# RWKV time mixing on one core: larger packets for the cast loads, and one store a batch for batches 2 to 9

## The chip, the cores and the metric

The kernel runs on one core of a Trainium2 chip. The metric is the device time of one execution in microseconds; for the kernel before it is the median of three runs, 203.77 us (203.05 to 205.11). The profile is of one execution of 203.05 us. Its span, from the first to the last instruction, is 201.3 us. All places in time below are counted from the start of that span.

## The reference: what is computed

The input x has 16 batches of 2048 rows of 256 float32 values. Each row is mixed with the row before it by three vectors of weights, projected by 256 x 256 matrices, gated by a sigmoid and projected once more:

```python
x_prev[:, 1:, :] = x[:, :-1, :]          # zero for the first row of a batch
xv = x * time_mix_v + x_prev * (1 - time_mix_v)
xr = x * time_mix_r + x_prev * (1 - time_mix_r)
v = xv @ value_weight
r = xr @ receptance_weight
out = (1 / (1 + exp(-r)) * v) @ output_weight
```

The reference also computes a key projection that does not reach the output; the kernel leaves it out. x is 33.55 MB, and so is the output: 2 MB each way for a batch.

## The kernel before

A batch is four units of 512 rows, so there are 64 units. For each unit the kernel brings x into the layout with the features on partitions (xt), mixes it with its shifted copy (mix), and multiplies: receptance (psum_r), value (psum_v), then, one unit later, the output projection of the gated product (psum_o). Each of these is a few matmuls on TensorE. ScalarE takes the sigmoid, copies the transposed x out of PSUM (xt) and copies the finished output (o_sb). VectorE adds and multiplies, GpSimd scales. The last 18 units and two blocks of batch 11 get their xt from DMA transposes, not from TensorE.

The buffers that matter here:

```python
xpool = ctx.enter_context(tc.tile_pool(name="xpool", bufs=6))
...
opool = ctx.enter_context(tc.tile_pool(name="opool", bufs=3))
ps_t_pool = ctx.enter_context(tc.tile_pool(name="ps_t", bufs=2, space=bass.MemoryType.PSUM))
ps_v_pool = ctx.enter_context(tc.tile_pool(name="ps_v", bufs=1, space=bass.MemoryType.PSUM))
ps_r_pool = ctx.enter_context(tc.tile_pool(name="ps_r", bufs=1, space=bass.MemoryType.PSUM))
ps_o_pool = ctx.enter_context(tc.tile_pool(name="ps_o", bufs=1, space=bass.MemoryType.PSUM))
...
x_unit = opool.tile([P, 3, UJ, D], FP32, name="o_sb")   # the first user of an output buffer
```

So six batches of x (bf16) can be in the core at once, and three batches of output (float32). An output buffer is taken by x_unit first, and then by the batches in turn: batch 0 takes the second, batch 1 the third, batch 2 the one of x_unit, batch 3 that of batch 0, batch 4 that of batch 1.

The loads. They cast from float32 to bf16 on the way and are issued by GpSimd. In batches 2 to 15 a partition holds 16 neighbouring rows of x, which are 16 KB in a row in memory; `max_dma_last_dim=8192` cuts them into two packets. Batches 0 and 1 are laid out by units (4 KB in a row).

```python
def rows(b):
    return x[b].rearrange("(p j) d -> p j d", p=P)

def unit_rows(t, b, e, n=1):
    return t[b, e * TU : (e + n) * TU, :].rearrange("(e p j) d -> p e j d", p=P, j=UJ)

def load(b):
    if b not in x_bf:
        x_bf[b] = xpool.tile([P, J, D], BF16, name="x_bf")
    if b < BYUNIT:                     # BYUNIT = 2
        for e in range(UB):
            nc.gpsimd.dma_start(
                out=x_bf[b][:, e * UJ : (e + 1) * UJ, :], in_=unit_rows(x, b, e)[:, 0]
            )
        return
    return nc.gpsimd.dma_start(out=x_bf[b], in_=rows(b), max_dma_last_dim=8192)
```

When loads go out. The load of batch b + 5 is issued where batch b begins to be transposed:

```python
            if b == 1 and e > 0:
                load(b + e + 1)
            elif b > 1 and e == 0 and b + 5 < B:
                if b == 2:
                    load(6)
                last_load = load(b + 5)
```

The output of a unit, and its store on SyncE. In batches 0 and 1 two units go out in one DMA, in pieces of 4 KB; after that two units go out in pieces of 8 KB; the last eight units go out one by one or in parts:

```python
def store(queue, b, lo, hi):
    dst = out[b].rearrange("(p j) d -> p j d", p=P)
    queue.dma_start(out=dst[:, lo:hi, :], in_=o_sb[b][:, lo:hi, :])

def output(g, z):
    b, e = divmod(g, UB)               # UB = 4 units a batch
    if e == 0:
        o_sb[b] = opool.tile([P, J, D], FP32, name="o_sb")
    j0 = e * UJ
    if g >= NU - 4:
        ...                            # the last units, in parts
        return
    ps = ps_o_pool.tile([P, UJ, D], FP32, name="psum_o")
    for jj in range(UJ):
        out_matmuls(ps, z, jj, jj)
    nc.scalar.copy(out=o_sb[b][:, j0 : j0 + UJ, :], in_=ps)     # line 335
    if b < BYUNIT:
        if e % 2 == 1:
            nc.sync.dma_start(
                out=unit_rows(out, b, e - 1, 2),
                in_=o_sb[b][:, j0 - UJ : j0 + UJ, :].rearrange("p (e j) d -> p e j d", j=UJ),
            )
    elif g >= NU - 8:
        store(nc.sync, b, j0, j0 + UJ)
    elif e % 2 == 1:
        store(nc.sync, b, j0 - UJ, j0 + UJ)
```

The order in the loop over units, cut to what matters. CROSS is 40:

```python
for g in range(NU - 1):
    ...
    project(ps_r, g, 0)                # receptance
    nc.scalar.activation(out=s_sb, in_=ps_r, func=ACT.Sigmoid)
    if g == CROSS:
        for e in (1, 2):
            by_dma(B - 5, e * UJ, (e + 1) * UJ, last_load)      # DMA transposes, after the last load
    advance(...)                       # loads and transposes of later units
    ...
    project(ps_v, g, 1)                # value
    nc.vector.tensor_tensor(out=z_sb, in0=s_sb, in1=ps_v, op=ALU.mult)
    ...
    output(g - 1, z_prev)              # from g = 41 on: output(g - 2), ahead of the value part
```

Of the kernel before, what the change touches and what calls it, by code (L numbers as in the profile page):

```python
# [15 lines left out]
def kernel(  # L16
# [25 lines left out]
    nc = tc.nc  # L42
# [4 lines left out]
    J = S // P  # L47
    UJ = 4
    TU = UJ * P
    UB = J // UJ  # L50
# [5 lines left out]
    CROSS = NU - BYDMA - LOOK  # L56
# [23 lines left out]
    x_bf = {}  # L80
# [12 lines left out]
# [13 lines that stand above are left out]
                    out=x_bf[b][:, e * UJ : (e + 1) * UJ, :], in_=unit_rows(x, b, e)[:, 0]  # L106
                )
            return
        return nc.gpsimd.dma_start(out=x_bf[b], in_=rows(b), max_dma_last_dim=8192)  # L109

    x_unit = opool.tile([P, 3, UJ, D], FP32, name="o_sb")
    tm_rows = consts.tile([2 * KO, P], FP32)
# [1 line left out]
    for m, tm in enumerate([time_mix_r, time_mix_v]):  # L114
        nc.scalar.dma_start(
            out=tm_rows[m * KO : (m + 1) * KO, :], in_=tm.rearrange("(ko p) -> ko p", p=P)
        )
    for h in (1, 0):
        nc.sync.dma_start(
            out=x_unit[:, 0, h * H : (h + 1) * H], in_=unit_rows(x, 0, 0)[:, 0, h * H : (h + 1) * H, :]  # L120
        )
    nc.sync.dma_start(
        out=w_f32[:, 0], in_=receptance_weight.rearrange("(ko p) n -> p ko n", p=P)
# [12 lines left out]
    nc.gpsimd.dma_start(out=x_bf3, in_=unit_rows(x, 0, 3)[:, 0])  # L136
    nc.gpsimd.dma_start(out=wo_bf, in_=output_weight.rearrange("(ko p) n -> p ko n", p=P))
    load(1)
    load(2)

    def warm_up(n):
# [159 lines left out]
    def out_matmuls(ps, z, jj, slot):  # L301
        for ko in range(KO):
            nc.tensor.matmul(  # L303
                out=ps[:, slot, :],
                lhsT=z[:, ko, jj * P : (jj + 1) * P],
                rhs=wo_bf[:, ko, :],
                start=(ko == 0),
                stop=(ko == KO - 1),
# [6 lines that stand above are left out]
    def out_part(pool, name, z, b, e, jj, n, copy, queue):  # L315
        ps = pool.tile([P, n, D], FP32, name=name)
        for k in range(n):
            out_matmuls(ps, z, jj + k, k)
        lo = e * UJ + jj
        copy(out=o_sb[b][:, lo : lo + n, :], in_=ps)  # L320
        store(queue, b, lo, lo + n)

    def output(g, z):
        b, e = divmod(g, UB)
# [4 lines that stand above are left out]
            for h, (pool, name) in enumerate([(ps_t_pool, "ps_t"), (ps_o_pool, "psum_o")]):  # L329
                out_part(pool, name, z, b, e, h * H, H, nc.scalar.copy, nc.sync)  # L330
# [4 lines that stand above are left out]
        nc.scalar.copy(out=o_sb[b][:, j0 : j0 + UJ, :], in_=ps)  # L335
# [5 lines that stand above are left out]
                )  # L341
        elif g >= NU - 8:
            store(nc.sync, b, j0, j0 + UJ)
        elif e % 2 == 1:
            store(nc.sync, b, j0 - UJ, j0 + UJ)

# [68 lines left out]
    def advance(limit):  # L415
        nonlocal tnext, last_load
        while tnext <= min(limit, NU - 1):
            b, e = divmod(tnext, UB)
# [6 lines that stand above are left out]
            if tnext < NU - BYDMA:  # L425
                transposes(tnext)
            tnext += 1

    first_transposes()
    for ko in range(KO):  # L430
        nc.vector.tensor_scalar(
            out=w_prev[:, ko, :],
# [6 lines left out]
        out=w_bf[:, 0, 0, :], in0=w_f32[:, 0, 0, :], scalar1=tms[:, 0, 0:1], scalar2=None, op0=ALU.mult  # L439
    )  # L440
    nc.scalar.activation(
        out=w_bf[:, 0, 1, :], in_=w_f32[:, 0, 1, :], func=ACT.Copy, scale=tms[:, 0, 1:2]
# [3 lines left out]
    for ko in range(KO):  # L446
        nc.vector.tensor_scalar(
            out=w_bf[:, 1, ko, :],
# [50 lines left out]
    for g in range(NU - 1):  # L499
# [23 lines left out]
        if LATE_O < g < NU - 2:  # L523
            output(g - 2, z_prev2)
# [29 lines left out]
        if z_prev is not None and not LATE_O <= g < NU - 3:  # L554
            output(g - 1, z_prev)
# [34 lines left out]
```

## Time and profile before

| | us |
|---|---|
| time, median of three runs | 203.77 |
| span in the profile | 201.3 |
| TensorE matmuls busy | 195.9 (97%) |
| VectorE busy | 186.7 (93%) |
| ScalarE busy | 180.9 (90%) |
| GpSimd busy | 83.3 (41%) |
| 14 loads of a batch (1024 KB of bf16 each): issue to landing, median | 27.1 |
| 28 stores of 1024 KB: issue to landing, median | 9.5 |

The busy time of an engine is the time in which one of its instructions was under way; matmuls overlap, so a busy TensorE can still be short of its peak. The page's second part cuts the span into 40 slices of 5 us and gives each a digit in tenths. The waits list, per engine and line, what ended an engine's idle time, with the total, the number of times and the longest one. A store's or load's time to landing runs from its issue to the last of its bytes, so it holds the time in the queue as well. Sizes of loads are those written, in bf16; as many bytes again are read, since the source is float32.

### The profile page before, as it was taken

The page shows a single profiled execution, that of the slowest core. Times are in us where ns is not written, and L with a number is a line of the kernel's source. Part 1 is how long each engine was busy: PE and PEld are TensorE (multiplying, and loading weights), DVE is VectorE, ACT ScalarE, POOL GpSimd, SP SyncE. Part 2 cuts the span into 40 slices and gives each one's busy share as a digit, 9 for nine tenths or more (in the row PEclk, how much of TensorE's full clock was granted, in tenths as well). Part 3 has the DMA queues.
Part 4 walks back from the last instruction along what each step waited for, and adds up shares of the span by engine and source line. Part 5 has one row for each costly group of instructions (what it writes and reads, how often), then busy time and mean ns, then how long its engine had stood idle before and what let it go on. Part 6 is the DMA issues. An engine that isn't in the chain of part 4 may idle for free.

```text
span 201.3 us, 3922 instructions
## 1 busy us (share of the span) xinstructions
PE 195.9 (97%) x1436; PEld 127.1 (63%) x1436; DVE 186.7 (93%) x301; ACT 180.9 (90%) x202; POOL 83.3 (41%) x109
## 2 busy tenths in 40 slices
PE   7999999999999999999999999999999999999992
PEld 7766676666666666666666666665656565555671
DVE  2899999999999999999999999999999999999963
ACT  2699899999999999999999999989999999999982
POOL 1754543462542644434462543434344444444200
PEclk9999999999999999999999999999999999999999
DMA  5999999999999999999999999989999999997575
GB/s 187 282 177 217 237 281 274 276 283 273 298 313 309 315 311 304 291 316 298 289 295 291 300 313 295 300 310 181 297 170 405 241 349 254 280 417 314 212 311 210
DMA packets 31130, 56.74 MB, mean 282 GB/s; under 512 B 19716, under 2 KB 21000, under 8 KB 28040
## 3 DMA queue, kind: packets, MB, share of 16 engines
q1 hardware_dynamic: 26160, 40.24, 59.2%
q0 software_dynamic: 4800, 16.12, 40.5%
q8 instruction: 11, 0.18, 0.3%
q10 hardware_dynamic: 152, 0.13, 0.2%
q14 instruction: 7, 0.06, 0.1%
HBM read 34.34 MB, written 33.55 MB: 337 GB/s over the span
## 4 chain that ended last, share of the span: by engine, by line
PE 83%; ACT 5%; DMA 5%; issue 3%; DVE 2%; SPq 0%; POOL 0%; DVEq 0%; ACTq 0%
PE psum_o L303 25%; PE psum_v L279 24%; PE psum_r L279 24%; PE ps_t L200 8%; DMA x_bf<-in_x_dram 3%; DMA w_f<-n_receptance_weight_dram 2%; ACT s_sb L512 2%; ACT mix L491 1%; ACT o_sb L335 1%; ACT xt L216 1%; DVE mix L271 1%; DVE z_sb L549 1%; DVE mix L249 1%; PE ps_t L303 1%; PE ps_t L279 0%
## 5 line engine op out<-in xcount | busy, mean ns | idle before, releaser
L259 POOL TENSOR_SCALAR mix<-xt,c_sb 128x1024 bf16<-128x1024 bf16 (+1 forms) x55 | 61.0, 1109 | 91.8 <-DVE mix L271 80.9
L549 DVE TENSOR_TENSOR z_sb<-s_sb,psum_v 128x1024 bf16<-128x1024 bf16 x63 | 76.6, 1217 | 3.6 <-PE psum_v L279 1.5
L271 DVE TENSOR_TENSOR mix<-mix,xt 128x1024 bf16<-128x1024 bf16 x112 | 77.3, 698 | 1.7
L279 PEld LDWEIGHTS <-w_bf 128*128 128x128 bf16 x516 | 48.7, 98 | 37.9 <-issue 0.7
L512 ACT ACTIVATE s_sb<-psum_r 128x1024 bf16<-128x1024 f32 x63 | 65.0, 1032 | 3.4 <-PE psum_r L279 2.7
L335 ACT COPY o_sb<-psum_o 128x1024 f32<-128x1024 f32 x60 | 61.1, 1018 | 7.5 <-PE psum_o L303 7.5
L279 PE MATMUL psum_v<-mix,w_bf 128*128 128x512 bf16 (+1 forms) x256 | 65.3, 377 | 0.3 <-DVE z_sb L549 0.2
L303 PE MATMUL psum_o<-wo_bf,z_sb 128*128 128x256 bf16 x494 | 64.4, 272 | 0.1
L279 PE MATMUL psum_r<-mix,w_bf 128*128 128x512 bf16 (+1 forms) x252 | 64.3, 377 | 0.1
L303 PEld LDWEIGHTS <-z_sb 128*128 128x128 bf16 x512 | 49.9, 98 | 20.7 <-issue 1.5
L216 ACT COPY xt<-ps_t 128x1024 bf16<-128x1024 bf16 x38 | 38.7, 1029 | 0.0
L200 PEld LDWEIGHTS <-x_bf 128*128 128x128 bf16 x344 | 22.5, 98 | 9.7 <-POOL xt_first L407 0.7
L200 PE MATMUL ps_t<-ident,x_bf 128*128 128x128 bf16 x344 | 25.7, 219 | 0.2 <-DMA x_bf<-in_x_dram 0.2
L249 DVE TENSOR_SCALAR mix<-xt,c_sb 128x1024 bf16<-128x1024 bf16 (+1 forms) x50 | 22.5, 459 | 0.0
L491 ACT ACTIVATE mix<-xt,c_sb 128x1024 bf16<-128x1024 bf16 x11 | 12.7, 1158 | 0.0
L109 POOL DMA_DIRECT2D x_bf<-in_x_dram x14 | 10.5, 749 | 0.0
L271 DVE TENSOR_TENSOR mix<-mix,xt_first 128x1024 bf16<-128x1024 bf16 x15 | 10.2, 686 | 0.1
L259 POOL TENSOR_SCALAR mix<-xt_first,c_sb 128x512 bf16<-128x512 bf16 x6 | 4.1, 686 | 8.3 <-DVE xt_first L408 8.2
L249 DVE TENSOR_SCALAR mix<-xt_first,c_sb 128x512 bf16<-128x512 bf16 x22 | 6.7, 355 | 0.2
L216 ACT COPY xt_first<-ps_t 128x1024 bf16<-128x1024 bf16 x5 | 5.1, 1029 | 0.0
L144 PE MATMUL ps_t<-zeros 128*128 128x128 bf16 x31 | 3.7, 313 | 1.0 <-DVE zeros L87 1.0
L144 PEld LDWEIGHTS <-zeros 128*128 128x128 bf16 x31 | 3.3, 148 | 1.0 <-DVE zeros L87 1.0
(64 smaller groups left out, 48.4 us busy)
## 6 DMA issues: line engine op xcount, KB each, us to landing
out_dram<-o_sb SPq DMA_DIRECT2D x28, 1024.0 KB, 9.5
x_bf<-in_x_dram POOLq DMA_DIRECT2D x14, 1024.0 KB, 27.1
out_dram<-o_sb SPq DMA_DIRECT2D x4, 512.0 KB, 2.7
out_dram<-o_sb SPq DMA_DIRECT2D x6, 256.0 KB, 2.5
x_bf<-in_x_dram POOLq DMA_DIRECT2D x5, 256.0 KB, 6.9
o_sb<-in_x_dram SPq DMA_DIRECT2D x2, 512.0 KB, 4.8
o_sb<-in_x_dram SPq DMA_DIRECT2D x2, 256.0 KB, 2.9
out_dram<-o_sb SPq DMA_DIRECT2D x3, 128.0 KB, 2.0
```

Of the source, the lines that this page charges most:

```text
L109: return nc.gpsimd.dma_start(out=x_bf[b], in_=rows(b), max_dma_last_dim=8192)
L200: nc.tensor.transpose(out=ps[:, jj], in_=src[:, jj, ko * P : (ko + 1) * P], identity=idn)
L216: nc.scalar.copy(out=xt[b][:, j0 : j0 + UJ], in_=ps)
L249: nc.vector.tensor_scalar(out=mixed(piece)[:, :, ko], in0=xt[b][:, slots(piece), ko], scalar1=c_sb[:, m, ko : ko + 1], scalar2=None, op0=A ...
L259: op = nc.gpsimd.tensor_scalar(out=mixed(piece)[:, :, 1], in0=xt[b][:, slots(piece), 1], scalar1=c_sb[:, m, 1:2], scalar2=1.0, op0=ALU.mul ...
L271: return nc.vector.tensor_tensor(out=mixed(piece), in0=mixed(piece), in1=xt[b][:, slots(piece, 1)], op=ALU.add)
L279: nc.tensor.matmul(out=ps[:, mo, :], lhsT=w_bf[:, m, ko, mo * P : (mo + 1) * P], rhs=mixed((b, m, e * TU + lo, e * TU + hi))[:, :, ko], st ...
L303: nc.tensor.matmul(out=ps[:, slot, :], lhsT=z[:, ko, jj * P : (jj + 1) * P], rhs=wo_bf[:, ko, :], start=(ko == 0), stop=(ko == KO - 1),)
L335: nc.scalar.copy(out=o_sb[b][:, j0 : j0 + UJ, :], in_=ps)
L491: nc.scalar.activation(out=mixed(piece)[:, :, ko], in_=xt[b][:, slots(piece), ko], func=ACT.Copy, scale=c_sb[:, m, ko : ko + 1],)
L512: nc.scalar.activation(out=s_sb, in_=ps_r, func=ACT.Sigmoid)
L549: nc.vector.tensor_tensor(out=z_sb, in0=s_sb, in1=ps_v, op=ALU.mult)
```

## The change

The loads of batches 2 to 15 are no longer cut: a partition's 16 KB go in one packet (8 KB written). The outputs of batches 2 to 9 are stored once a batch, when the last of its four units has been copied, so that a partition's 16 KB go in one packet as well. The purpose is to have fewer and larger packets, each of which has a fixed part of its own. Batches 0 and 1 and batches 10 to 15 are stored as before.

```diff
-        return nc.gpsimd.dma_start(out=x_bf[b], in_=rows(b), max_dma_last_dim=8192)
+        return nc.gpsimd.dma_start(out=x_bf[b], in_=rows(b), max_dma_last_dim=16384)
...
         elif g >= NU - 8:
             store(nc.sync, b, j0, j0 + UJ)
+        elif g < CROSS:
+            if e == UB - 1:
+                store(nc.sync, b, 0, J)
         elif e % 2 == 1:
             store(nc.sync, b, j0 - UJ, j0 + UJ)
```

## The prediction

> **What bounds the kernel now.** I read the page's busy shares first, then the chain that ended last, the waits, the DMA queues by stretch, and last the timeline around one output copy. From the page:
>
> ```profile
> PE 195.9 (97%) x1436; PEld 127.1 (63%) x1436; DVE 186.7 (93%) x301; ACT 180.9 (90%) x202; POOL 83.3 (41%) x109
> ...
> PEclk9999999999999999999999999999999999999999
> DMA  5999999999999999999999999989999999997575
> ...
> PE 83%; ACT 5%; DMA 5%; issue 3%; DVE 2%; SPq 0%; POOL 0%; DVEq 0%; ACTq 0%
> ```
>
> TensorE is busy for 97% of the span at full clock and carries 83% of the chain, so nothing can be gained where it already runs without a gap. But the second row of digits says that the DMA engines are full too, from 5 to about 180 us. In the waits, TensorE lost almost nothing to them:
>
> ```profile
> PE ps_t L200 <- DMA x_bf<-in_x_dram: 0.2, 1, 0.2
> ```
>
> So there are two full resources side by side, and DMA is hidden only by buffers: six for loads, three for outputs. The question is what the change does to the order in which the DMA engines serve the two queues, and whether a buffer then comes free too late. Here are the queues in two stretches, 36 to 48 us and 60 to 72 us (queue, packets, MB, share of 16 engines; q0 carries the loads issued on GpSimd, q1 the stores issued on SyncE):
>
> ```profile
> DMA packets 868, 3.34 MB, mean 278 GB/s; under 512 B 56, under 2 KB 56, under 8 KB 867
> q0 software_dynamic: 432, 1.67, 68.6%
> q1 hardware_dynamic: 435, 1.65, 36.3%
> ...
> q0 software_dynamic: 337, 1.27, 52.4%
> q1 hardware_dynamic: 335, 2.48, 51.2%
> ```
>
> In the first stretch the load packets (8 KB read, 4 KB written as bf16) meet the 4 KB stores of batches 0 and 1; in the second they meet the 8 KB stores of later batches. In both, the packet **counts** are equal (432 to 435, 337 to 335), while the shares of time are 2:1 and then 1:1. The engines take one packet of each queue in turn, whatever its size. This is the fact on which my prediction rests.
>
> The third reading is how late outputs and loads land. The store of the second half of batch 1 goes out at 39.7 us, and the load of batch 10 at 54.4 us:
>
> ```profile
> L338 SPq DMA_DIRECT2D out_dram<-o_sb x1: 373/373/373, 39.7 to 39.7; - x1
> DMA to landing us min/median/max: 14.8/14.8/14.8
> ...
> L109 POOL DMA_DIRECT2D x_bf<-in_x_dram x1: 757/757/757, 54.4 to 54.4; - x1
> DMA to landing us min/median/max: 36.4/36.4/36.4
> ```
>
> The store lands at 54.5 us. Its buffer's next user is the first output copy of batch 4 (three output buffers in rotation, x_unit being the first user of one):
>
> ```profile
> L335 ACTq EVENT_SEMAPHORE  x1: 38/38/38, 64.2 to 64.2; - x1
> ...
> 65.91 1.01 ACT L335 COPY o_sb<-psum_o 128x1024 f32<-128x1024 f32 x1 [0.20 <-PE psum_o L303]
> ...
> 67.88 1.04 PE L303 MATMUL psum_o<-wo_bf,z_sb 128*128 128x256 bf16 x8
> ```
>
> The wait instruction stands once per batch ahead of its first copy, so I take it to cover all stores from the old buffer. The copy starts at 65.91 us, 11.4 us after the store landed: that is today's margin. The third line is TensorE's next use of the same PSUM buffer, at 67.88 us. The copy ends at 66.92, so TensorE gives it only 0.96 us of slack.
>
> **What the Trainium skill says.** "DMA: Bandwidth & Descriptors", section Queues, rings and completion order: each DMA engine goes round its queue rows packet by packet. The trace agrees, with the counts above. That page puts several descriptors into a typical packet; here the equal counts show that the turn passes after each 4 or 8 KB piece. Section Rules for kernel authors of that page wants at least 1 MiB a DMA for bandwidth; the loads and most stores have that already, so there is little left to gain from larger ones. Section Issuing engines are not separate DMA queues: the queues run on the same 16 engines. The shares above, 68.6 and 36.3% in one stretch, agree.
>
> **The change part by part.** First the price of a packet. In 36 to 48 us, q0 has 1.67 MB in 4 KB pieces, 408 packets, for 68.6% of 16 x 12 us = 131.7 us: 323 ns each. q1 has 1.65 MB, 403 packets, for 69.7 us: 173 ns each. In 60 to 72 us, q1's 8 KB packets (2.48 MB, 303 packets, 98.3 us) take 324 ns. So 4 KB more costs 151 ns and a packet has some 22 ns of its own. Estimates for the new sizes from this: 626 ns for a 16 KB store; for a 16 KB load, twice the 8 KB load less one fixed part, 2 x 323 - 22 = 624 ns.
>
> 1. *Loads with half the packets.* A batch has 128 packets of 624 ns instead of 256 of 323: over 16 engines 4.99 us instead of 5.17. Gain 0.18 us a batch of DMA time. TensorE does not wait for loads, so this is worth nothing by itself. GpSimd's issue (750 ns each, 14 times) may shorten; GpSimd is 41% busy, so again nothing.
>
> 2. *Stores of batches 2 to 9 in one piece.* 128 packets of 626 ns instead of 256 of 324: 5.01 instead of 5.18 us of DMA time a batch, and one issue less. Against it the first half of a batch is sent two units, 6.1 us, later. Nothing waits for the early half alone. Worth nothing on the path either.
>
> 3. *What moves: who gets the engines.* A store packet now waits for a load packet of 624 instead of 323 ns. The stores of batches 0 and 1 are not changed: each batch lies as four unit blocks, so they stay at 4 KB, 256 packets a DMA, 16 per engine, 64 per engine for all four DMAs. Before, the second landed at 25.6 + 13.8 = 39.4 us and the fourth at 54.5: 32 turns in 15.1 us, 0.472 us a turn. One packet of each kind costs 323 + 173 = 496 ns, so engines overlap packets by 5%. Sixty-four turns are 30.2 us, which puts the effective start at 54.5 - 30.2 = 24.3 us. After: (624 + 173) / 1.05 = 0.759 us a turn, 64 turns are 48.6 us, landing at **72.9 us** instead of 54.5.
>
> That needs a load packet in the queue at every turn. A load is now 8 packets per engine, 6.1 us at this pace; the eight loads of batches 3 to 10 fill 64 turns. The last of them would start at 24.3 + 7 x 6.07 = 66.8 us and is issued at 54.4, so the loads never run dry before the stores are through. They get far ahead of need instead, at the stores' cost.
>
> 4. *The new wait.* The copy that starts at 65.91 us must now wait for 72.9 us. Add its 1.01 us: the PSUM buffer is free at about 73.9, and TensorE wanted it at 67.88. The loss is 73.9 - 67.9 = **6.0 us**. My start point folds in latency and the larger packets may overlap a little better, which could bring landing down to about 71.5 us and the loss to 4.6. I take 5.2 us. ScalarE is too full (11.19 of 12 us in this stretch) and TensorE completely full, so nothing is made up later.
>
> 5. *Does it happen again?* The store of batch 2 stands behind these, issued after the copy that starts at 50.68. Eight turns of (624 + 626) / 1.05 = 1.19 us end at 72.9 + 9.5 = 82.4. Batch 5's first copy needs that buffer at 78.10, by then moved to about 83.3. Just in time. Batch 3's store ends near 92 and is needed at 90.28 + 5.2 = 95.5. From there on margins grow, for a batch needs 5.0 + 5.0 us of DMA in 12.2 us of TensorE. One stall, not a chain of them.
>
> Sum: 0 + 0 + 5.2, on 203.77: 208.9 us.
>
> **The rivals.** *A. Hidden anyway, about 203.6 us:* the fourth store may land before 66 us, if the engines serve by bytes and not by packets, or if the buffer wait covers less than I think. For it: the margin of 11.4 us is not small. Against it: equal counts at two size ratios. *B. A gain, 201 to 203 us:* the last load (issued 115.2, landed 133.9) comes earlier, and the DMA transposes behind it start earlier; SyncE waited 2.6 us for it. Against: no engine waits for those transposes in the list of waits, and the slow place at 131 to 138 us is a run of ScalarE and VectorE work. *C. Later damage, 210 us or more:* batch 9's 2 MB store, now whole, goes out at about 138 us beside the DMA transposes, or batch 2's store is late as well. Each could cost 1 to 2 us; the transposes land 3 to 12 us after issue and still nobody waits, which speaks for slack.
>
> **Range and chances.** My main line runs from 208.4 to 210 us. Rival A has a quarter of the weight, with a partial stall between, so the range is 203.3 to 210.6. Two per cent slower is 207.85 us, a loss of 4.1 us: most of the main line lies above it, but closely. Faster by 2% would need 4.1 us from a TensorE that idles for 5.4 us in all, most of it at both ends.
>
> **What would show it.** Right: ScalarE idle about 5 us before a copy at line 335 near 66 to 72 us, released by a DMA of out_dram; the fourth store's time to landing near 32 us instead of 14.8; load landings shrunk early (batch 7's from 37.9 to under 30 us); equal packet counts in 36 to 48 us with shares near 3.6:1; TensorE at 3.05 us a unit elsewhere. Wrong: no such wait and store landings under 26 us (packets not served in turn), or several such waits in later batches (the backlog not drained), or TensorE waiting for x_bf or for xt after 140 us.

## The result, and the profile after

The changed kernel takes 210.6 us (median of six executions, 209.69 to 211.49) against 203.78 us before. The ratio is 1.0324, with a 95% interval of 1.0279 to 1.0369: slower by 3.2%.

From the page of the changed kernel, the lines that answer to those of before (busy shares, TensorE's clock and the DMA engines in 40 slices, the chain that ended last):

```profile
PE 197.4 (94%) x1436; PEld 127.1 (61%) x1436; DVE 186.6 (89%) x301; ACT 180.9 (87%) x202; POOL 80.1 (38%) x109
...
PEclk9999999999999969999999999999999999999999
DMA  5999999999999999998979889799999999977575
...
PE 59%; DMA 18%; DVE 9%; ACT 6%; issue 5%; SPq 1%; POOL 0%; DVEq 0%; ACTq 0%; POOLq 0%
```

The work of every engine is the same as before within about 3 us, but the span is 208.9 us instead of 201.3. DMA now holds 18% of the chain, and one slice, at 73 to 78 us, has a clock digit of 6 (the granted clock was 0.50 from 74 to 77 us). Some DMA digits between 94 and 136 us are lower than before: the backlog of transfers is gone by then, and the kernel is still slower. The list of waits says where (who waited for whom: total, times, longest):

```profile
ACT o_sb L335 <- DMA out_dram<-o_sb: 6.4, 1, 6.4
PE psum_o L303 <- ACT o_sb L335: 5.1, 1, 5.1
```

Both happen once. The DMA queues between 36 and 48 us (queue, packets, MB, share of 16 engines) show what came before:

```profile
DMA packets 553, 3.06 MB, mean 255 GB/s; under 512 B 50, under 2 KB 50, under 8 KB 309
q0 software_dynamic: 276, 2.00, 79.5%
q1 hardware_dynamic: 277, 1.06, 23.2%
```

The counts of the two queues are still equal, 276 and 277. The loads' packets are now 8 KB written, so the loads get 79.5% of the time instead of 68.6, and the 4 KB stores 23.2% instead of 36.3. Without the small packets, q0 has 2.00 MB in 244 packets of 8 KB, 626 ns each. The store of the second half of batch 1, by its issue and its time to landing:

```profile
L338 SPq DMA_DIRECT2D out_dram<-o_sb x1: 373/373/373, 40.3 to 40.3; - x1
...
DMA to landing us min/median/max: 32.3/32.3/32.3
```

It lands at 72.6 us, 32.3 us after its issue instead of 14.8. And the timeline around that moment (start, duration, engine, line, what; in brackets the idle time before and what ended it):

```profile
67.63 1.03 PE L279 MATMUL psum_v<-mix,w_bf 128*128 128x512 bf16 x4
...
72.70 1.01 ACT L335 COPY o_sb<-psum_o 128x1024 f32<-128x1024 f32 x1 [6.38 <-DMA out_dram<-o_sb]
...
73.76 1.86 PE L303 MATMUL psum_o<-wo_bf,z_sb 128*128 128x256 bf16 x8 [5.10 <-ACT o_sb L335]
...
75.42 1.87 PE L279 MATMUL psum_r<-mix,w_bf 128*128 128x512 bf16 x4
...
77.57 1.03 PE L279 MATMUL psum_v<-mix,w_bf 128*128 128x512 bf16 x4
```

ScalarE's first copy of batch 4 waits for the store, TensorE waits for the copy, and when TensorE goes on, its next two groups of matmuls take 1.86 and 1.87 us where 1.04 and 1.03 are usual. From the value matmuls of unit 18 to those of unit 19, this trace shows 67.63 to 77.57 us, 9.94 us. The trace of before shows the same pair 3.05 us apart:

```profile
67.02 1.03 PE L279 MATMUL psum_v<-mix,w_bf 128*128 128x512 bf16 x4
...
70.07 1.03 PE L279 MATMUL psum_v<-mix,w_bf 128*128 128x512 bf16 x4
```

The difference is 6.9 us: psum_o starts 6.13 us after the value matmuls instead of 0.86, which is 5.27 us, and the slow matmuls take the other 1.62 us. Of the 7.6 us between the spans, 0.7 us more lie in the start-up: VectorE's first product comes at 11.34 us instead of 10.61. The traces of all kernels here spread from 10.61 to 12.43 us at that point. From the product of unit 24 to that of unit 62 the two kernels take the same time, 106.77 and 106.76 us.

In what follows, the **cost of the stretch** is the time from VectorE's product of unit 17 to that of unit 24, less the 21.30 us that it takes in before. It is free of the start-up's spread. The changed kernel's is 93.94 - 65.74 - 21.30 = 6.90 us.

### The profile page after: what moved, and what is told of

Same layout as the page of the kernel before. It is cut to its first block, busy times and chain, and to the rows that moved or that the text cites. A ratio compares the mean times of both kernels' runs of the same rounds, so it can differ in the third digit from the quotient of the medians.

```text
span 208.9 us, 3906 instructions
## 1 busy us (share of the span) xinstructions
PE 197.4 (94%) x1436; PEld 127.1 (61%) x1436; DVE 186.6 (89%) x301; ACT 180.9 (87%) x202; POOL 80.1 (38%) x109
## 4 chain that ended last, share of the span: by engine, by line
PE 59%; DMA 18%; DVE 9%; ACT 6%; issue 5%; SPq 1%; POOL 0%; DVEq 0%; ACTq 0%; POOLq 0%
PE psum_o L303 19%; PE psum_r L279 18%; PE psum_v L279 17%; DMA out_dram<-o_sb 15%; PE ps_t L200 4%; DVE mix L271 4%; DMA w_f<-in_value_weight_dram 3%; DVE mix L249 3%; ACT o_sb L335 2%; ACT s_sb L515 2%; ACT xt L216 1%; ACT mix L494 1%; DVE z_sb L552 1%; DVE xt_first L411 1%; PE ps_t L303 1%
## 5 line engine op out<-in xcount | busy, mean ns | idle before, releaser
L303 PE MATMUL psum_o<-wo_bf,z_sb 128*128 128x256 bf16 x494 | 65.2, 275 | 5.2 <-ACT o_sb L335 5.1
L279 PE MATMUL psum_r<-mix,w_bf 128*128 128x512 bf16 (+1 forms) x252 | 65.1, 381 | 0.1
L271 DVE TENSOR_TENSOR mix<-mix,xt_first 128x1024 bf16<-128x1024 bf16 x15 | 10.1, 681 | 0.1
L109 POOL DMA_DIRECT2D x_bf<-in_x_dram x14 | 8.0, 573 | 0.0
L144 PE MATMUL ps_t<-zeros 128*128 128x128 bf16 x31 | 3.1, 282 | 1.0 <-DVE zeros L87 1.0
L209 ACT CAST xt_first<-ps_t 128x512 bf16<-128x512 f32 x4 | 2.1, 588 | 1.9 <-PE ps_t L200 1.9
```

Source lines behind the costliest of these rows:

```text
L271: return nc.vector.tensor_tensor(out=mixed(piece), in0=mixed(piece), in1=xt[b][:, slots(piece, 1)], op=ALU.add)
L279: nc.tensor.matmul(out=ps[:, mo, :], lhsT=w_bf[:, m, ko, mo * P : (mo + 1) * P], rhs=mixed((b, m, e * TU + lo, e * TU + hi))[:, :, ko], st ...
L303: nc.tensor.matmul(out=ps[:, slot, :], lhsT=z[:, ko, jj * P : (jj + 1) * P], rhs=wo_bf[:, ko, :], start=(ko == 0), stop=(ko == KO - 1),)
```

## The experiments

**The load half and the store half.** First the loads alone, on the kernel before:

```diff
-        return nc.gpsimd.dma_start(out=x_bf[b], in_=rows(b), max_dma_last_dim=8192)
+        return nc.gpsimd.dma_start(out=x_bf[b], in_=rows(b), max_dma_last_dim=16384)
```

> Only the load half of the change: 16 KB load packets, stores as before. If the unchanged 4 KB stores of batches 0 and 1 each wait a turn for a longer load packet, the fourth of them still lands near 72 us (32 us after issue) and the whole loss stays: 210 to 211 us, one wait of ScalarE for out_dram of about 6 us before batch 4. If instead the stores held back to one per batch are the cause, this is within 0.5% of before, about 203.8 us.

Measured: 211.88 us, ratio 1.0329 (1.0245 to 1.0413). Here and below the time is the median, and the ratio is estimated from the fast executions alone (here three of four), so it is not exactly the quotient of two medians. The list of waits and the fourth store's time to landing (issued at 41.5 us):

```profile
ACT o_sb L335 <- DMA out_dram<-o_sb: 6.6, 1, 6.6
PE psum_o L303 <- ACT o_sb L335: 5.3, 1, 5.3
...
DMA to landing us min/median/max: 32.5/32.5/32.5
```

The whole loss is here, with the same single wait; the cost of the stretch is 7.02 us. (The median is 0.9 us above the expected band; in this trace the first product came 1.1 us later than in the changed kernel's.) Then the stores alone:

```diff
+        elif g < CROSS:
+            if e == UB - 1:
+                store(nc.sync, b, 0, J)
         elif e % 2 == 1:
             store(nc.sync, b, j0 - UJ, j0 + UJ)
```

> Only the store half: one store a batch for batches 2 to 9, loads in 8 KB packets as before. By the theory of turns the fourth store lands at 54 to 55 us as before and the time is 203.8 us, within 0.5%. If the late, large stores cause the loss through the output buffers, it is 208 us or more, with ScalarE waiting for out_dram in batch 5 or later.

Measured: 204.31 us, ratio 1.0020 (0.9988 to 1.0053). The fourth store lands 15.3 us after its issue, the stretch costs 0.01 us, and no engine waits for out_dram. One store a batch neither helps nor harms.

**Take the wait away, leave the traffic.** The whole change, with a fourth output buffer:

```diff
-    opool = ctx.enter_context(tc.tile_pool(name="opool", bufs=3))
+    opool = ctx.enter_context(tc.tile_pool(name="opool", bufs=4))
```

> The whole change with four output buffers instead of three; the DMA traffic is the same until a buffer is reused. By the theory the fourth store still lands near 72 us, but its buffer is next used by batch 5 at 78 us, so nobody waits: 203.5 to 204 us, with TensorE at full clock throughout. If slower DMA service harms in another way (loads, memory, TensorE clock), the time stays above 206 us.

Measured: 204.39 us, ratio 1.0024 (0.9994 to 1.0054). The fourth store of this run:

```profile
L338 SPq DMA_DIRECT2D out_dram<-o_sb x1: 373/373/373, 40.1 to 40.1; - x1
...
DMA to landing us min/median/max: 32.7/32.7/32.7
```

It lands as late as in the changed kernel, at 72.8 us, and it costs nothing: the stretch costs 0.01 us. The lateness itself harms only through the buffer. The slow slice of the clock is gone too, so the slow matmuls followed the stop and not the transfers.

**Large packets only where no small store competes.** The whole change, but:

```diff
-        ... max_dma_last_dim=16384)
+        ... max_dma_last_dim=16384 if b >= 11 else 8192)
```

> The whole change, but the loads of batches 2 to 10 keep 8 KB packets and only batches 11 to 15 have 16 KB. By the theory the 4 KB stores meet only short load packets: fourth store at 54 to 56 us, 203.8 us. If 16 KB load packets harm at any time of the kernel, about a third of the loss remains: 206 us.

Measured: 203.76 us, ratio 0.9983 (0.9955 to 1.0011). The fourth store lands 15.4 us after its issue, the stretch costs nothing. With the harm gone, the rest of the change gains nothing that can be told from zero.

**A dose of it.** 16 KB packets in the loads up to batch 8, later up to batch 9:

```diff
-        ... max_dma_last_dim=16384)
+        ... max_dma_last_dim=16384 if b <= 8 else 8192)      # then: b <= 9
```

> A dose of the cause: the whole change, with 16 KB packets only in the loads of batches 2 to 8. By turns, the loads of batches 3 to 8 fill 48 long turns of 0.76 us and the last 16 turns are 0.47 us, so the fourth store lands at 24.3 + 36.5 + 7.6 = 68.4 us; TensorE loses 68.4 + 1.1 - 67.9 = 1.6 us, plus some fraction of the 1.9 us that the slower clock after the stall cost: 205.4 to 207 us. If the loss does not depend on the number of long turns, it is 210.6 or 203.8.

Measured: 204.94 us, ratio 1.0052 (1.0032 to 1.0071). The store lands 26.6 us after its issue at 41.1, at 67.7 us; ScalarE waits 0.7 us, less than TensorE's slack of 0.96, and the stretch costs 0.01 us. The expected landing was 68.4 us by the clock of the trace of before. Here the units, and the store's issue with them, ran 1.4 us later than there, so against the copy the store is some 2 us earlier than the turns say, and the expected 1.6 us of loss did not come about. The records of single packets in this trace give a reason. Between the first and the last packet of the four stores, from 24.2 to 66.6 us, the engines served 680 load packets of 8 KB written and 285 of 4 KB. That is 42.5 long turns for each of the 16 engines instead of 48: the other 88 of the 768 packets of batches 3 to 8 had gone before the first store packet. At 0.284 us a turn (0.756 less 0.472) this is worth 1.6 of the 2 us.

> The next dose: 16 KB packets in the loads of batches 2 to 9. With loads to batch 8 the fourth store landed at 67.7 us, where the copy would have started at 67.0; eight more long turns of 0.756 instead of 0.472 us put landing at 70.0 us. ScalarE waits 3.0 us; TensorE, with 0.96 us of slack, idles 2.0 us. If the slow clock follows any idling of TensorE, another 1 to 1.9 us are lost: 206.5 to 207.6 us; if a stop of 2 us does not trigger it, 205.8 us. If the number of long turns did not set the loss, it is 204.9 or 210.6.

Measured: 208.06 us, ratio 1.0226 (1.0189 to 1.0264). Its trace is of the fastest execution, 206.51 us:

```profile
69.93 1.01 ACT L335 COPY o_sb<-psum_o 128x1024 f32<-128x1024 f32 x1 [4.01 <-DMA out_dram<-o_sb]
70.99 1.03 PE L303 MATMUL psum_o<-wo_bf,z_sb 128*128 128x256 bf16 x8 [2.74 <-ACT o_sb L335]
```

The median lies above both of the expected times. The store landed at 69.9 us, 70.0 was expected, but this execution began 1.2 us earlier than the one from which I had reckoned. So ScalarE waited 4.0 us instead of 3.0. TensorE stood still for 2.74 us and went on at full speed (1.03 us), and the stretch costs 2.95 us. Of the other three executions two took 208.6 us with a mean clock of 0.992, the third 207.5 with 0.997. So a stop of this length seems to lie at the edge of what slows TensorE. That reading rests on mean clocks, not on traces of those executions. The dose can be read from the wait before the copy, less the 0.2 us that ScalarE idles there in any case: with 16 KB loads up to batch 8 it is 0.5 us, up to batch 9 3.8, in all batches 6.2, and with none the store landed 11.4 us early. Counted as above, the long load packets served among the four stores are 680, 845, 949 and none. From none to 949 the store moves by 17.6 us against the copy, about 18.5 ns a packet; a turn longer by 284 ns on one of 16 engines is 17.8. So the number of long turns ahead of the store sets its landing.

> The kernel with 16 KB load packets up to batch 8 again, in more rounds. Its trace lost nothing between units 17 and 24 (the wait of 0.7 us fits into TensorE's slack of 0.96), yet its times were 0.5% above before. If the 0.5% is real it is here again, and some executions wait longer than the traced one; if it is the spread of the start-up, the interval includes 1.

Measured: 204.85 us, ratio 1.0058 (1.0035 to 1.0081). The 0.5% is there again. The trace has ScalarE waiting 1.2 us, half a microsecond more than the first trace of this kernel, and a stretch that costs 0.14 us. The rest of its span's excess lies before the first product, at 12.22 us, where nothing differs from before. Whether that is a real effect of this kernel or not stays open.

**The same stall without any large packet.** The kernel before, with its loads, but the stores of batches 0 and 1 in 2 KB packets:

```diff
-                nc.sync.dma_start(
-                    out=unit_rows(out, b, e - 1, 2), in_=...)
+                for u in (e - 1, e):
+                    nc.sync.dma_start(
+                        out=unit_rows(out, b, u)[:, 0],
+                        in_=o_sb[b][:, u * UJ : (u + 1) * UJ, :],
+                        max_dma_last_dim=2048,
+                    )
```

> The kernel before, loads in 8 KB packets, but the stores of batches 0 and 1 cut into 2 KB packets (and one DMA a unit, both of a pair issued together). Twice the turns, each 323 + 90 ns over 1.05 = 0.39 us: 128 turns are 50 us, landing at 74 to 75 us, so the same kind of stall with no large packet at all: TensorE loses 7 to 8 us and about 2 us to the clock, 211 to 214 us. If engines share by bytes, or if large load packets are what harms, the time is 203.8 us.

Measured: 210.87 us, ratio 1.0341 (1.0303 to 1.0380). The queues between 36 and 48 us, and the wait:

```profile
q0 software_dynamic: 514, 1.99, 81.8%
q1 hardware_dynamic: 514, 0.99, 24.3%
```

```profile
ACT o_sb L335 <- DMA out_dram<-o_sb: 5.6, 1, 5.6
```

Equal counts once more, 514 and 514, now with 4 KB written against 2 KB. The last store lands at 72.8 us; the stretch costs 6.18 us. TensorE stood still for 4.3 us, not 7 to 8: the store landed 1 to 2 us sooner than expected, and the units ran 1.5 us later than in the trace of before. So the same stall comes without any 16 KB packet, with load and store packets again at two to one (this run also issues each pair of units as two DMAs). What harms is the ratio between the two queues' packets. Larger packets in both queues at once, which would keep the ratio of before, were not tried.

**The other direction.** The kernel before with `max_dma_last_dim=4096` in the loads:

> The kernel before with 4 KB load packets (173 ns each), the other direction. By turns the stores gain: 64 turns of 0.33 us from 24.3 us, so the fourth store lands about when the queue allows it, 45 to 47 us instead of 54.5, and the loads of batches 3 and 4 lose: batch 3 lands near 33 us instead of 30.9, batch 4 near 44 instead of 38.5, just before they are needed. Time 203.8 us, or up to 1.5 us more if TensorE waits for batch 4's load.

Measured: 204.44 us, ratio 1.0030 (1.0009 to 1.0051). The queues between 24 and 28 us, while both had work, and two waits:

```profile
q1 hardware_dynamic: 197, 0.81, 53.4%
q0 software_dynamic: 198, 0.41, 53.4%
```

```profile
POOL mix L259 <- DMA xt<-x_bf: 2.0, 1, 2.0
...
PEld L200 <- DMA x_bf<-in_x_dram: 0.5, 1, 0.5
```

The second and the fourth store land 11.0 and 10.2 us after issue instead of 13.8 and 14.8, the fourth at 50.8 us; between them their queue ran nearly empty, which my 45 to 47 us had left out. Now the loads are the ones that come late: TensorE's weight load waits 0.5 us for batch 3's load, and GpSimd 2.0 us for a DMA transpose, which stands behind the last load. From unit 24 to unit 62 it takes 107.12 us instead of 106.76, so a little is lost on that side.

**The slow clock.** The changed kernel, with zero matmuls where TensorE stands still (into a PSUM tile of the transposes' pool):

```diff
+        if g == 18:
+            warm_up(90)
         if z_prev is not None and not LATE_O <= g < NU - 3:
             output(g - 1, z_prev)
```

> The changed kernel with 90 matmuls of zeros (128 columns each, about 4.8 us at full clock) put where TensorE waits for the output copy of batch 4. If the slow matmuls after the stall (1.86 and 1.66 us where 0.87 is usual) come from TensorE having been idle, they run at full rate now and the kernel takes about 1.9 us less than the changed one: 208.7 us. If the slow clock has another cause, it stays at 210.6 us or above.

Measured: 209.94 us, ratio 1.0297 (1.0255 to 1.0339). The timeline of the stall:

```profile
69.39 5.19 PE L144 MATMUL ps_t<-zeros 128*128 128x128 bf16 x90
72.98 1.01 ACT L335 COPY o_sb<-psum_o 128x1024 f32<-128x1024 f32 x1 [5.76 <-DMA out_dram<-o_sb]
...
74.42 1.04 PE L303 MATMUL psum_o<-wo_bf,z_sb 128*128 128x256 bf16 x8
...
75.29 1.03 PE L279 MATMUL psum_r<-mix,w_bf 128*128 128x512 bf16 x4
```

The matmuls after the stall run at full rate, 1.04 and 1.03 us, the mean clock is 1.000 instead of 0.992, and the stretch costs 92.97 - 66.64 - 21.30 = 5.03 us, 1.87 less than in the changed kernel. Of these, 1.62 us are the slow matmuls that are gone. ScalarE's wait was 0.62 us shorter in this execution, and 0.4 us of that went again, for the zero matmuls ended that much after the copy. The expected 208.7 us did not come: the medians differ by only 0.7 us, which their spread does not separate. In the trace, the start-up came 0.9 and the tail 0.6 us later than in the changed kernel's. So what shows the cause of the slow clock is the trace, not the total time.

## Why the prediction was right, step by step

The prediction was 208.9 us, the time is 210.6. The mechanism is the predicted one, and its main links have runs of their own; one term of the sum was missing. The time lies above the main line of 208.4 to 210 us and exactly at the upper end of the range, so that the range holds it by luck: it had no allowance for the missing term.

- **Packets are served in turn:** shown. Equal counts at four pairs of sizes (written): 4 to 4 KB and 4 to 8 KB before, 8 to 4 KB after, 4 to 2 KB with the small stores; and 2 to 4 KB with the small loads while both queues had work.
- **Price of a packet, 624 ns:** 626 measured. **A turn, 0.759 us:** the second and the fourth store land at 48.4 and 72.6 us, 24.2 us for 32 turns, 0.756.
- **Landing at 72.9 us:** 72.6, in an execution whose stores and units ran 0.6 us later than in the trace of before. By the clock of before that is 72.0, 0.9 us sooner than worked out and inside the allowance made (71.5).
- **TensorE's loss by the wait, worked out as 6.0 and then taken as 5.2 us:** 5.27 until psum_o starts, the 6.0 less most of the 0.9 us by which the store landed sooner. That the 5.2 comes so close is partly luck, for it was a choice between 4.6 and 6.0.
- **Nothing is made up later:** right, 106.77 against 106.76 us from unit 24 to unit 62.
- **One stall and not a chain:** right. The store of batch 2 landed at 52.3 + 30.1 = 82.4 us, as worked out, and the first copy of batch 5 came at 85.6. The store of batch 3 landed at 87.3 us, not near 92: TensorE's stop held back the load of batch 12 to 86.1 us, and from 82.7 us, when the one before it had landed, the stores had the engines to themselves.
- **Loads and stores gain nothing by themselves:** right. GpSimd's issue of a load fell from 750 to 573 ns, the loads land earlier (those issued at 25 to 26 us after 22.1 and 27.7 us instead of 28.8 and 37.9), and the runs with the stores alone and with late large loads are at 1.002 and 0.998.
- **What was missing:** the step of the new wait took the loss to be the standstill alone. TensorE also ran slowly after it, at a cost of 1.6 us in that trace; with zero matmuls in the stop this cost was gone. With 5.2 + 1.6 us the sum would have been 210.6. The Trainium skill has this: "TensorE: Matmul & The Clock Gate", section Part 1: The HAM clock gate, says that the clock falls to half after an idle window of about 3.4 us and comes back after as long a busy one. The traces agree: the granted clock was 0.50 for about 3.4 us after the stop of 5.10 us, stops of 4.3 to 5.3 us were followed by slow matmuls in the traces of all three kernels in which nothing filled them, and one of 2.74 us was not.

Of the rivals, A (hidden anyway) fell with the first trace. B (a gain from an earlier last load) did not appear: in the run with late large loads the last one lands 10.1 us after issue instead of 18.7, and nothing is gained. C (later damage by batch 9's whole store) did not appear: no compute engine waits for a DMA after the stall.

## What to carry to other kernels

Where two DMA queues are busy at once, compare the sizes of their packets before enlarging one of them: in these traces the queues took turns packet by packet, so that each got engine time roughly in proportion to the time of its packet (79.5 to 23.2% here, with 626 and 173 ns), and the small-packet transfers landed later though nothing about them was changed. Then look for the buffer that waits for them, and for its margin. When a change will make TensorE stand still for several microseconds (4.3 us and more here), add the slow matmuls after the stop to the sum, some 1.6 us in these runs.

## What the runs showed that I had not expected

That a single stop of 4.3 to 5.3 us costs TensorE another 1.5 to 1.7 us, and that the same late store, 32.7 us from issue to landing, costs nothing measurable with one more output buffer.
